# One core, one layer: the forgetting gate moved into the second score product, and four smaller edits

## The chip, the core and the metric

The kernel runs on one core of one Trainium2 chip. The metric is device time in microseconds, from the program's start to its end. Three runs of the kernel before took 779.17, 785.84 and 786.11 us, so the median is 785.84 us. A core has a matmul engine (PE, whose weight loads are listed apart as PEld), a vector engine (DVE), a scalar engine (ACT), GpSimd (POOL) and a queue engine (SP), and each works through its own list of instructions in order.

## The reference

One layer of a streaming encoder on 512 positions of width 1024, in float32. Three sub-layers, each with an RMS norm before and after it: a token mixer, cross-attention into 256 memory rows, and a SwiGLU block of width 2816. The mixer has 8 heads of forgetting attention (fox) and 8 heads of chunked attention with a learned relative bias. The change touches the fox heads and the SwiGLU block.

```python
# fox head: q, k, v are 512 x 64; log_f is the logarithm of a sigmoid gate, one per head and position
c = cumsum(log_f)
s = q @ k.T / 8 + c[:, None] - c[None, :]          # and -1e30 where the key is later than the query
p = softmax(s); out = p @ v
# SwiGLU
g, u = split(h @ w_gate_up)                          # 1024 -> 2 x 2816
y = (silu(g) * u) @ w_down
```

## The kernel before

**Two-part numbers.** Every large product is made of float32 values held as a high part (rounded to the PE's fast format) and a low part (the rest). `mm3` (lines 139 to 142) issues three matmuls for one product: high by high (L140), high by low (L141) and low by high (L142). ACT makes the high parts and DVE the low parts, also of all weights that arrive by DMA.

**Order.** The Python code is written in the order of the algorithm, and a scheduler puts the instructions of each engine in order, by a priority that runs on with the code. `later(n)` shifts the priority of what stands in it, so that one stage's work is drawn between another's. The built program has one fixed list per engine; a wait holds up all that stands behind it on that engine.

**Stages.** The first stage (0 to 35 us) computes V of the fox heads while x and its weights arrive: `x_block`, `v_weights` and `squares` prepare 128 rows of features at a time, `v_products` uses them. The loop at L237 gives PE six small matmuls on a zeroed tile before any data is there. Sums of squares run over POOL (L289) and DVE (L321, L322). `vhi` and `vlo` hold the weights, in a part of 264 columns and one of 256 columns.

**Heads.** Four groups of four heads follow (35 to 245 us). `group_proj` computes Q and K of a group; its matmuls are PE's filler between the steps of the heads. `fin_q` writes Q with the high part of a head in one half of the 128 rows (`own`) and the low part in the other (`other`). `fin_k` writes T with the high part of K in both halves, and L with the low part of K in `own` and zeros in `other` (the zeros come from POOL, L383 and L384, once for each of three tiles in `klz`). So a head's score is two matmuls: Q by T (L515) gives high by high and low by high, and Q by L (L516) gives high by low. `forget_gate` computes c for all eight heads, as high and low rows in `c40`, and its columns in `ct`. `fox_bias` then makes, for each fox head, one matmul that spreads the row -c over 128 partitions (L480), four ACT steps that add the column c (L485) and four POOL steps that write the causal mask (L486). `head` adds that bias to the score while it looks for the row's maximum (DVE, L519), exponentiates (ACT, L529), divides (L530, L531), transposes (PE, L534), splits into two parts again (L536, L537) and multiplies by V (L543).

**SwiGLU.** Blocks of 256 columns of gate and up, u = 0 to 10. Block 0 is `first_ffn`. Of the others, three halves run as `eight` (eight plain products of 128x512x256) and seventeen as `seven` (seven products of sums, Strassen's way). `product` is the common piece: four times `mm3` with 256 columns. Weights pass through a ring (`ring_hi`, `ring_lo`, lines 902 and 903) that `take` fills as far ahead as its slots are free. The down projection follows (663 to 775 us). There, `mm` can cut the third matmul of one `mm3` in two (`cuts`, L1226 to L1229), which happens once in each half:

```python
            for part in (slice(0, cut), slice(cut, to.stop - to.start)):
                pe.matmul(dst[:, part], lhs[1], rhs[0][:, part], start=False, stop=end)
```

## Time and profile before

| | |
|---|---|
| runs shown | 779.17, 785.84, 786.11 us |
| profiled execution | 786.02 us, span 784.1 us from the first to the last instruction |
| PE busy | 763.6 us (97%), 4996 matmuls |
| DVE, ACT, POOL busy | 597.9, 429.7, 70.9 us |
| chain that ended last | PE 81%, ACT 6%, DVE 5% |

A matmul's record is longer than the time it takes from its neighbours, because matmuls overlap: 256 columns show as 0.28 us, but the next one starts after 0.11 or 0.12 us. So PE's speed is read from the starts, or from the number of matmuls in a stretch. The profiled execution is close to the median of the runs.

### The profile page before, as it was taken

The page shows a single profiled execution, that of the slowest core. Times are in us where ns is not written, and L with a number is a line of the kernel's source. Part 1 is how long each engine was busy: PE and PEld are TensorE (multiplying, and loading weights), DVE is VectorE, ACT ScalarE, POOL GpSimd, SP SyncE. Part 2 cuts the span into 40 slices and gives each one's busy share as a digit, 9 for nine tenths or more (in the row PEclk, how much of TensorE's full clock was granted, in tenths as well). Part 3 has the DMA queues.
Part 4 walks back from the last instruction along what each step waited for, and adds up shares of the span by engine and source line. Part 5 has one row for each costly group of instructions (what it writes and reads, how often), then busy time and mean ns, then how long its engine had stood idle before and what let it go on. Part 6 is the DMA issues. An engine that isn't in the chain of part 4 may idle for free.

```text
span 784.1 us, 12865 instructions
## 1 busy us (share of the span) xinstructions
PE 763.6 (97%) x4996; PEld 683.5 (87%) x4996; DVE 597.9 (76%) x1089; ACT 429.7 (55%) x781; POOL 70.9 (9%) x110
## 2 busy tenths in 40 slices
PE   8899999999999999999999999999999999999996
PEld 8887788888778988877778899999999999898985
DVE  5567889879887588645563778998899998987736
ACT  7358888757886348444553635554344446454421
POOL 6001231110321101000001100000000000000001
PEclk9999999999999999999999999999999999999999
DMA  6241212412312734421350202332433332323222
GB/s 245 79 137 54 55 55 67 130 67 82 114 60 96 276 107 163 131 72 64 107 171 18 81 28 81 108 109 81 135 109 108 108 109 77 111 92 124 89 74 107
DMA packets 60748, 80.05 MB, mean 102 GB/s; under 512 B 2704, under 2 KB 43664, under 8 KB 60688
## 3 DMA queue, kind: packets, MB, share of 16 engines
q1 hardware_dynamic: 59264, 74.49, 29.5%
q0 software_dynamic: 1280, 4.72, 1.6%
q8 instruction: 39, 0.64, 0.3%
q14 instruction: 21, 0.17, 0.1%
q10 hardware_dynamic: 144, 0.02, 0.0%
HBM read 77.13 MB, written 2.10 MB: 101 GB/s over the span
## 4 chain that ended last, share of the span: by engine, by line
PE 81%; ACT 6%; DVE 5%; issue 3%; DMA 2%; POOL 2%; SPq 0%; DVEq 0%; POOLq 0%; ACTq 0%
PE ps_a L141 15%; PE ps_a L142 15%; PE ps_a L140 15%; PE ps_s L140 5%; PE ps_s L141 5%; PE ps_s L142 5%; PE ps_t L141 2%; PE ps_t L140 2%; PE ps_t L142 2%; PE ps_o L140 2%; PE ps_o L141 2%; PE ps_o L142 2%; PE ps_t L534 2%; DMA raw<-in_dram 2%; PE ps_o L543 2%
## 5 line engine op out<-in xcount | busy, mean ns | idle before, releaser
L902 ACT CAST ring_hi<-fraw 128x1024 fp32r<-128x1024 f32 (+1 forms) x62 | 57.5, 931 | 65.1 <-DVE fraw L981 16.2
L126 DVE TENSOR_TENSOR lo<-raw,hi 128x1024 fp32r<-128x1024 f32 x56 | 68.2, 1223 | 22.2 <-ACT hi L125 21.8
L903 DVE TENSOR_TENSOR ring_lo<-fraw,ring_hi 128x1024 fp32r<-128x1024 f32 (+1 forms) x62 | 66.4, 1074 | 18.4 <-ACT ring_hi L902 17.9
L142 PE MATMUL ps_a<-hTh,lo 128*128 128x512 f32 x192 | 76.8, 400 | 0.6 <-DVE lo L126 0.6
L140 PE MATMUL ps_a<-hTh,hi 128*128 128x512 f32 x192 | 75.8, 395 | 0.2 <-ACT hi L125 0.2
L141 PE MATMUL ps_a<-hTl,hi 128*128 128x512 f32 x192 | 75.9, 395 | 0.0
L125 ACT CAST hi<-raw 128x1024 fp32r<-128x1024 f32 x56 | 57.8, 1048 | 23.8 <-PE ps_a L141 15.0
L902 ACT CAST ring_hi<-sums 128x1024 fp32r<-128x1024 f32 x34 | 35.7, 1049 | 52.5 <-PE ps_t L141 17.0
L903 DVE TENSOR_TENSOR ring_lo<-sums,ring_hi 128x1024 fp32r<-128x1024 f32 x34 | 41.4, 1218 | 4.0 <-ACT ring_hi L902 4.0
L142 PEld LDWEIGHTS ps_a<-hTh,lo 128*128 128x128 f32 x192 | 36.1, 188 | 7.3 <-DVE lo L126 1.0
L141 PEld LDWEIGHTS ps_a<-hTl,hi 128*128 128x128 f32 x192 | 36.1, 188 | 6.4
L140 PEld LDWEIGHTS ps_a<-hTh,hi 128*128 128x128 f32 x192 | 36.2, 188 | 6.0 <-ACT hi L125 0.4
L529 ACT ACTIVATE p<-p,nm 128x128 f32<-128x128 f32 (+1 forms) x64 | 36.1, 565 | 8.4 <-DVE nm L519 7.6
L140 PE MATMUL ps_a<-b,ring_hi 128*128 128x256 f32 x140 | 39.4, 281 | 0.0
L141 PE MATMUL ps_a<-b,ring_hi 128*128 128x256 f32 x140 | 39.3, 281 | 0.0
L142 PE MATMUL ps_a<-b,ring_lo 128*128 128x256 f32 x140 | 39.3, 281 | 0.0
L140 PE MATMUL ps_s<-b,ring_hi 128*128 128x256 f32 x128 | 36.0, 281 | 0.0
L141 PE MATMUL ps_s<-b,ring_hi 128*128 128x256 f32 x128 | 36.0, 281 | 0.0
L142 PE MATMUL ps_s<-b,ring_lo 128*128 128x256 f32 x128 | 36.0, 281 | 0.0
L536 ACT CAST pth<-ps_t 128x128 fp32r<-128x128 f32 (+1 forms) x64 | 27.1, 425 | 14.5 <-PE ps_t L534 13.7
L537 DVE TENSOR_TENSOR ptl<-ps_t,pth 128x128 fp32r<-128x128 f32 (+1 forms) x64 | 30.7, 486 | 5.1 <-ACT pth L536 3.8
L534 PE MATMUL ps_t<-ident,p 128*128 128x128 f32 x160 | 28.1, 275 | 1.1 <-DVE p L531 0.8
(541 smaller groups left out, 2642.5 us busy)
## 6 DMA issues: line engine op xcount, KB each, us to landing
raw<-in_dram SPq DMA_DIRECT2D x64, 512.0 KB, 3.7
fraw<-in_dram SPq DMA_DIRECT2D x62, 512.0 KB, 3.5
cb<-in_dram SPq DMA_DIRECT2D x8, 256.0 KB, 2.7
xo<-in_dram POOLq DMA_DIRECT2D x4, 512.0 KB, 5.4
out_dram<-yd SPq DMA_DIRECT2D x8, 256.0 KB, 2.0
rawv<-in_dram SPq DMA_DIRECT2D x3, 520.0 KB, 6.9
xt<-in_dram SPq DMA_DIRECT2D x3, 512.0 KB, 7.7
gb<-in_dram POOLq DMA_DIRECT2D x3, 512.0 KB, 4.4
```

Of the source, the lines that this page charges most:

```text
L125: act.copy(hi[:, j : j + n, :], raw)
L126: dve.tensor_tensor(out=lo[:, j : j + n, :], in0=raw, in1=f32(hi[:, j : j + n, :]), op=ALU.subtract)
L140: pe.matmul(dst, sh, mh, start=first, stop=False)
L141: pe.matmul(dst, sh, ml, start=False, stop=False)
L142: pe.matmul(dst, sl, mh, start=False, stop=last)
L529: act.activation(p[:, :n], p[:, :n], AF.Exp, bias=nm, scale=-1.0, accum_out=sm)
L534: pe.transpose(tp[:, k * P : (k + 1) * P], p[:, k * P : (k + 1) * P], ident)
L536: act.copy(span(ph, i), t3)
L537: dve.tensor_tensor(out=span(pl, i), in0=t3, in1=f32(span(ph, i)), op=ALU.subtract)
L543: pe.matmul(acc[:, a:], v[:, k, vh, :], m[:, k * PTS + a : k * PTS + SEQ], start=k == 0 and m is ph, stop=k == NT - 1 and m is pl,)
L902: act.copy(h2, v)
L903: dve.tensor_tensor(out=l2, in0=v, in1=f32(h2), op=ALU.subtract)
```

## The change

The diff makes five edits.

1. The gate goes into the second score product. The zero half of L takes the rows of `c40` (`gate_rows`, ACT), and the left operand of that product becomes a new tile `ql` (`fox_left`): the high part of Q in `own`, and in `other` a column of -1 in the rows that hold this head's c (two ACT steps of 64x512 for each head). The column c is left out, since the softmax of a row doesn't depend on it. One causal mask serves all heads. `fox_bias`, `ct` and its transposes are gone. The zeros of L are written when the chunked heads need them.
2. The loop before the data arrives has ten matmuls in place of six.
3. The 256-column part of `vhi` and `vlo` starts 48 elements into its tile.
4. ACT uses Exp once right after the gate's Ln, and Silu once at the end of cross-attention.
5. In gate blocks u = 1, 2, 4 and 7, the third matmul of the first `product` is cut into two of 128 columns.

```diff
-        for j in range(6):
+        for j in range(10):
...
-        vhi = [wp.tile([P, KB, n], F32R, tag="hi", name=f"vhi{n}", bufs=2) for n in (264, 256)]
-        vlo = [wp.tile([P, KB, n], F32R, tag="lo", name=f"vlo{n}", bufs=2) for n in (264, 256)]
+        def v_part(tag, n, skip):
+            t = wp.tile([P, skip + KB * n], F32R, tag=tag, name=f"v{tag}{n}", bufs=2)
+            return t[:, skip:].rearrange("p (k n) -> p k n", k=KB)
+
+        vhi, vlo = ([v_part(tag, n, skip) for n, skip in ((264, 0), (256, AS_MOVING))] for tag in ("hi", "lo"))
...
-            pool.memset(f32(l[H1, 0, :]), 0.0)
-            pool.memset(f32(l[H0, 1, :]), 0.0)
...
+                if 4 < nkl[0] <= 4 + len(klz):
+                    pool.memset(f32(l[H1, 0, :]), 0.0)
+                    pool.memset(f32(l[H0, 1, :]), 0.0)
...
+            act.activation(warm, u[:, :1], AF.Exp)
...
-            sel = cst.tile([P, 8], F32R, tag="sel", name="sel")
-            pool.memset(f32(sel), 0.0)
-            for r in (0, 32):
-                dve.tensor_scalar(
...
-            ct = cst.tile([P, NT, 8], F32, tag="ct", name="ct")
...
-                pe.transpose(tp[:, t * 8 : (t + 1) * 8], c[:, t * P : (t + 1) * P], ident[0:8, 0:8])
-            dve.tensor_copy(ct, tp[:, : NT * 8].rearrange("p (t h) -> p t h", t=NT))
-            return c40, sel, ct
 
-        def fox_bias(h, c40, sel, ct):
-            acc = bank("s")
-            pe.matmul(acc, sel[:, h : h + 1].to_broadcast([P, P]), c40, start=True, stop=True)
...
-                t = bp.tile([P, SEQ], F32, tag="bi", name=f"fb{h}_{i}", bufs=4)
-                act.activation(t[:, :n], acc[:, :n], AF.Identity, bias=ct[:, i, h : h + 1])
-                pool.affine_select(
...
-                tiles.append(t[:, :n])
-            return tiles
+            return c40
...
+        sel = cst.tile([P, 8], F32, tag="sel", name="sel")
+        dve.memset(sel, 0.0)
+        for r in (0, 32, 64, 96):
+            dve.tensor_scalar(
+                out=sel[r : r + 8, :], in0=ident[r : r + 8, r : r + 8], scalar1=-1.0, scalar2=None, op0=ALU.mult
+            )
+        causal = bp.tile([P, SEQ], F32, tag="causal", name="causal")
+        pool.memset(causal, 0.0)
+        pool.affine_select(
...
+        masks = [causal[:, SEQ - (i + 1) * P :] for i in range(NT)]
+
+        def gate_rows(l, c40, h):
+            act.copy(l[(H1, H0)[h], h, :], c40[H0, :])
+
+        def fox_left(q, h, hh):
+            own, other = ((H0, H1), (H1, H0))[h]
+            t = bp.tile([P, SEQ], F32R, tag="bi", name=f"ql{hh}", bufs=4)
+            act.copy(t[own, :], f32(q[own, h, :]))
+            act.activation(t[other, :], ones[other, :].to_broadcast([64, SEQ]), AF.Copy, scale=sel[other, hh : hh + 1])
+            return t
...
-        def head(q, kt, kl, v, vh, h, bias, o):
+        def head(q, ql, kt, kl, v, vh, h, bias, o):
...
                 pe.matmul(s[:, :w], q[:, h, ts], kt[:, h, :w], start=True, stop=False)
-                pe.matmul(s[:, :w], q[:, h, ts], kl[:, h, :w], start=False, stop=True)
+                pe.matmul(s[:, :w], ql[:, ts], kl[:, h, :w], start=False, stop=True)
...
-                        bias = fox_bias(hh, *gate) if side == 0 else chunk_bias(hh)
+                        if n == 0 and b == 0:
+                            gate_rows(klz[0], gate, h)
+                        if side == 0:
+                            bias, ql = masks, fox_left(q[b], h, hh)
+                        else:
+                            bias, ql = chunk_bias(hh), q[b][:, h, :]
+                    if n == 0 and h == 1:
+                        with later(urge[n]):
+                            for other in range(2):
+                                gate_rows(klz[b + 1], gate, other)
                     with later(urge[n]):
-                        head(q[b], kt[b], kl[b], v, 2 * b + h, h, bias, o)
+                        head(q[b], ql, kt[b], kl[b], v, 2 * b + h, h, bias, o)
...
+        act.activation(mix_ms[:, 0, 0:1], sm[:, :1], AF.Silu)
...
-        def product(dst, w, b, first=True, last=True):
+        def product(dst, w, b, first=True, last=True, parts=(slice(0, 256),)):
             for k in range(4):
-                mm3(dst, w[0][:, k, :], w[1][:, k, :], b[:, 0, k, :], b[:, 1, k, :], first and k == 0, last and k == 3)
+                if k:
+                    parts = (slice(0, 256),)
+                pe.matmul(dst, w[0][:, k, :], b[:, 0, k, :], start=first and k == 0, stop=False)
+                pe.matmul(dst, w[0][:, k, :], b[:, 1, k, :], start=False, stop=False)
+                for to in parts:
+                    pe.matmul(dst[:, to], w[1][:, k, :], b[:, 0, k, to], start=False, stop=last and k == 3)
+        IN_STEP = (slice(0, P), slice(P, 256))
...
-                        product(accs[m][:, ns], w, bs[n], half == 0 and n == 0, half == 1 and n == 1)
+                        begin = half == 0 and n == 0
+                        product(accs[m][:, ns], w, bs[n], begin, half == 1 and n == 1, *([parts] if begin and m == 0 else []))
...
-            product(p17[:, left], a11, b11)
+            product(p17[:, left], a11, b11, parts=parts)
...
+            whole, parts = (slice(0, 256),), IN_STEP if u in (1, 2, 4, 7) else (slice(0, 256),)
             if 2 * u in EIGHT:
-                eight(("a", "a"), gate_eight)
+                eight(("a", "a"), gate_eight, parts)
             else:
-                seven(G, ("a", "a", "a", "o"), gate_seven)
+                seven(G, ("a", "a", "a", "o"), gate_seven, parts)
...
             else:
-                seven(U, ("s", "s", "t", "t"), up_seven(dst))
+                seven(U, ("s", "s", "t", "t"), up_seven(dst), whole)
```

The built lists show the change at three places. The first is POOL in the first stage, from the zeroing of L to the last sum of squares (`xs`). Before:

```order
L383 MEMSET L_412 64x512
L384 MEMSET L_412 64x512
L289 TENSOR_TENSOR xs<-xs 128x512
L383 MEMSET L_415 64x512
L289 TENSOR_TENSOR xs<-xs 128x512
L384 MEMSET L_415 64x512
L383 MEMSET L_418 64x512
L289 TENSOR_TENSOR xs<-xs 128x512
L384 MEMSET L_418 64x512
L289 TENSOR_TENSOR xs<-xs 128x512
L454 MEMSET fzero 8x512
```

Now:

```order
L478 MEMSET causal 128x512
L459 MEMSET fzero 8x512
L292 TENSOR_TENSOR xs<-xs 128x512
L479 AFFINE_SELECT causal<-causal 128x128
L292 TENSOR_TENSOR xs<-xs 128x512
L463 MEMSET c_615 128x512
L292 TENSOR_TENSOR xs<-xs 128x512 x2
```

Between the second and the last of the sums, four zeroing steps of L have gone, and one mask step (`causal`) and the zeroing of `c40` stand there.

The second place is PE and ACT at the first fox head. `ps_s` are scores, `ps_a` the projection that fills in. PE before:

```order
L480 MATMUL ps_s_624<-c_605,sel 128x512
L515 MATMUL ps_s_646<-T_542,Q_468 128x256
L516 MATMUL ps_s_646<-L_412,Q_468 128x256
L142 MATMUL ps_a_1042<-hTh,lo_506 128x512
L140 MATMUL ps_a_1074<-hTh,hi_505 128x512
L141 MATMUL ps_a_1074<-hTl,hi_505 128x512
L142 MATMUL ps_a_1074<-hTh,lo_506 128x512
L140 MATMUL ps_a_1074<-hTh,hi_505 128x512
L141 MATMUL ps_a_1074<-hTl,hi_505 128x512
L515 MATMUL ps_s_661<-T_542,Q_468 128x256
L516 MATMUL ps_s_661<-L_412,Q_468 128x256
L142 MATMUL ps_a_1074<-hTh,lo_506 128x512
```

and now:

```order
L140 MATMUL ps_a_1003<-hTh,hi_514 128x512
L141 MATMUL ps_a_1003<-hTl,hi_514 128x512
L518 MATMUL ps_s_627<-L_416,ql_624 128x256
L518 MATMUL ps_s_642<-L_416,ql_624 128x256
L142 MATMUL ps_a_1003<-hTh,lo_515 128x512
L140 MATMUL ps_a_1003<-hTh,hi_514 128x512
L517 MATMUL ps_s_658<-T_551,Q_477 128x384
L518 MATMUL ps_s_658<-L_416,ql_624 128x384
L141 MATMUL ps_a_1003<-hTl,hi_514 128x512
L142 MATMUL ps_a_1003<-hTh,lo_515 128x512
L140 MATMUL ps_a_1003<-hTh,hi_514 128x512
```

The matmul L480 is gone, Q by T of the first two tiles has moved ahead (it isn't shown), and L by `ql` waits for ACT's rows. ACT before:

```order
L459 CAST c_605<-fc 8x512
L485 ACTIVATE fb_0_626<-ps_s_624,ct 128x128
L485 ACTIVATE fb_1_631<-ps_s_624,ct 128x256
L485 ACTIVATE fb_2_636<-ps_s_624,ct 128x384
L485 ACTIVATE fb_3_641<-ps_s_624,ct 128x512
L529 ACT_TABLE_LOAD
L529 ACTIVATE p_0_649,sm_651<-p_0_649,nm_650 128x128
L406 ACTIVATE Q_1069<-qk 64x512 x2
L529 ACTIVATE p_1_664,sm_666<-p_1_664,nm_665 128x256
```

and now:

```order
L464 CAST c_615<-fc 8x512
L491 COPY L_416<-c_615 64x512 x2
L491 COPY L_417<-c_615 64x512
L531 ACTIVATE p_0_630,sm_632<-p_0_630,nm_631 128x128
L491 COPY L_417<-c_615 64x512
L491 COPY L_418<-c_615 64x512
L531 ACTIVATE p_1_645,sm_647<-p_1_645,nm_646 128x256
L538 CAST pth_408<-ps_t_638 128x128
L491 COPY L_418<-c_615 64x512
L497 ACTIVATE ql_1114<-ones,sel 64x512
```

In place of four bias steps and a table load stand six copies of the gate's rows, three of them ahead of the first exponential.

The third place is PE at the start of gate block u = 2 (`b` is the activation, `ring` the weights). Before:

```order
L142 MATMUL ps_s_4961<-b_4272,ring_lo 128x256
L140 MATMUL ps_a_5072<-b_4271,ring_hi 128x256
L141 MATMUL ps_a_5072<-b_4271,ring_hi 128x256
L142 MATMUL ps_a_5072<-b_4271,ring_lo 128x256
L140 MATMUL ps_a_5072<-b_4271,ring_hi 128x256
L141 MATMUL ps_a_5072<-b_4271,ring_hi 128x256
L142 MATMUL ps_a_5072<-b_4271,ring_lo 128x256
```

and now:

```order
L1086 MATMUL ps_s_4822<-b_4132,ring_lo 128x256
L1083 MATMUL ps_a_4933<-b_4131,ring_hi 128x256
L1084 MATMUL ps_a_4933<-b_4131,ring_hi 128x256
L1086 MATMUL ps_a_4933<-b_4131,ring_lo 128x128 x2
L1083 MATMUL ps_a_4933<-b_4131,ring_hi 128x256
L1084 MATMUL ps_a_4933<-b_4131,ring_hi 128x256
L1086 MATMUL ps_a_4933<-b_4131,ring_lo 128x256
```

The third matmul has become two of 128 columns; nothing else moved there. At u = 4 and 7 it is the same. At u = 1 four transposes stand between the halves, and the rest of block 0's matmuls come after them.

## Rows read from the trace of the kernel before

**Rows 1.** The page: busy time of each engine, and the chain that ended last

```profile
PE 763.6 (97%) x4996; PEld 683.5 (87%) x4996; DVE 597.9 (76%) x1089; ACT 429.7 (55%) x781; POOL 70.9 (9%) x110
...
PE 81%; ACT 6%; DVE 5%; issue 3%; DMA 2%; POOL 2%; SPq 0%; DVEq 0%; POOLq 0%; ACTq 0%
```

**Rows 2.** Windows: stretch, its length, busy time and count by engine, granted clock, DMA

```profile
60.00:150.00 90.00, 87.28 (x491) 72.61 (x490) 76.69 (x209) 75.91 (x176) 18.51 (x41) 1.00 0.25 71
483.85:663.34 179.49, 179.49 (x1526) 179.49 (x1525) 164.43 (x238) 87.84 (x132) 0.00 (x0) 1.00 0.32 103
564.41:643.43 79.02, 79.02 (x673) 79.02 (x672) 74.77 (x108) 37.40 (x56) 0.00 (x0) 1.00 0.33 105
686.20:708.90 22.70, 22.70 (x203) 22.70 (x202) 18.58 (x30) 12.37 (x18) 0.00 (x0) 1.00 0.34 116
```

**Rows 3.** Timeline of PE, first stage: start, length, what, idle before and its end

```profile
1.05 2.93 PE L237 MATMUL ps_t<-rrow 128*128 128x128 f32 x12 [1.05 <-DVE mhalf L82]
...
5.67 0.78 PE L140 MATMUL ps_s<-vhi,hTh 128*128 128x264 f32 x2 [1.70 <-DVE vhi L271]
...
20.27 0.39 PE L141 MATMUL ps_s<-vlo,hTh 128*128 128x264 f32 x1 [1.06 <-DVE vlo L275]
```

**Rows 4.** Timeline of POOL and of DVE, first stage

```profile
17.11 0.52 POOL L384 MEMSET L<- 64x512 f32 x1
17.59 1.28 POOL L289 TENSOR_TENSOR xs<-xs 128x512 f32<-128x512 f32 x1
...
15.27 0.73 DVE L281 SCALAR_TENSOR_TENSOR hTl<-xt,gn,hTh 128x512 fp32r<-128x512 f32 x1
18.91 0.69 DVE L322 TENSOR_TENSOR xs<-xs 128x512 f32<-128x512 f32 x1 [2.90 <-POOL xs L289]
```

**Rows 5.** Timeline of PE at the first fox head

```profile
59.79 0.41 PE L474 MATMUL ps_t<-ident,fc 8*128 8x8 f32 x4 [0.30 <-DVE fc L456]
60.13 0.50 PE L142 MATMUL ps_a<-hTh,lo 128*128 128x512 f32 x1
...
64.34 0.40 PE L480 MATMUL ps_s<-c,sel 128*128 128x512 f32 x1
64.58 0.28 PE L515 MATMUL ps_s<-T,Q 128*128 128x256 f32 x1
...
69.01 0.50 PE L515 MATMUL ps_s<-T,Q 128*128 128x512 f32 x1 [1.22 <-DVE nm L519]
```

**Rows 6.** Timeline of ACT at the first fox head

```profile
64.78 1.78 ACT L485 ACTIVATE fb<-ps_s,ct 128x128 f32<-128x128 f32 x4 [1.96 <-PE ps_s L480]
66.58 1.28 ACT L529 ACT_TABLE_LOAD   x1
67.88 0.40 ACT L529 ACTIVATE p<-p,nm 128x128 f32<-128x128 f32 x1
```

**Rows 7.** Lines L485 and L422 on ACT: count, ns least, median and most

```profile
L485 ACT ACTIVATE fb<-ps_s,ct x32: 346/524/717, 64.8 to 133.0; 128x128 f32<-128x128 f32 x8, 128x256 f32<-128x256 f32 x8, 128x384 f32<-128x384 f32 x8, 128x512 f32<-128x512 f32 x8
...
L422 ACT CAST T<-qk x16: 607/618/622, 53.2 to 209.4; 64x512 fp32r<-64x512 f32 x16
```

**Rows 8.** Waits of PE for the bias: us in total, times, longest

```profile
PE ps_s L515 <- ACT fb L485: 1.0, 2, 0.7
```

**Rows 9.** Timeline of PE in block 0 of SwiGLU

```profile
455.45 0.41 PE L141 MATMUL ps_a<-b,gate_w 128*128 128x256 f32 x2
455.70 0.28 PE L142 MATMUL ps_a<-b,gate_w 128*128 128x256 f32 x1
```

**Rows 10.** Timeline of PE at the cut in the down projection

```profile
685.25 0.28 PE L1227 MATMUL ps_s<-ring_lo,latex 128*128 128x256 f32 x1
685.36 0.33 PE L1229 MATMUL ps_s<-ring_hi,latex 128*128 128x128 f32 x2
...
685.82 0.28 PE L142 MATMUL ps_s<-ring_hi,latex 128*128 128x256 f32 x1
685.94 0.28 PE L140 MATMUL ps_a<-ring_hi,latex 128*128 128x256 f32 x1
```

More of the change, by code (lines that the diff above doesn't have):

```diff
@@ L472, in forget_gate @@
-            tp = bank("t")
-            for t in range(NT):
-                pe.transpose(tp[:, t * 8 : (t + 1) * 8], c[:, t * P : (t + 1) * P], ident[0:8, 0:8])
-            dve.tensor_copy(ct, tp[:, : NT * 8].rearrange("p (t h) -> p t h", t=NT))
-            return c40, sel, ct
-        def fox_bias(h, c40, sel, ct):
-            acc = bank("s")
-            pe.matmul(acc, sel[:, h : h + 1].to_broadcast([P, P]), c40, start=True, stop=True)
-            tiles = []
-            for i in range(NT):
-                n = (i + 1) * P
-                t = bp.tile([P, SEQ], F32, tag="bi", name=f"fb{h}_{i}", bufs=4)
-                act.activation(t[:, :n], acc[:, :n], AF.Identity, bias=ct[:, i, h : h + 1])
-                pool.affine_select(
-                    out=t[:, i * P : n],
-                    in_=t[:, i * P : n],
-                    pattern=[[-1, P]],
-                    compare_op=ALU.is_ge,
-                    fill=NEG,
-                    base=0,
-                    channel_multiplier=1,
-                )
-                tiles.append(t[:, :n])
-            return tiles
+            return c40
@@ new lines, in hybrid_block_kernel @@
+        sel = cst.tile([P, 8], F32, tag="sel", name="sel")
[7 more added lines that the diff above has]
+        pool.affine_select(
+            out=causal[:, SEQ - P :],
+            in_=causal[:, SEQ - P :],
+            pattern=[[-1, P]],
+            compare_op=ALU.is_ge,
+            fill=NEG,
+            base=0,
+            channel_multiplier=1,
+        )
@@ L1081, in up_eight, with eight @@
             return done
-        def eight(tags, done):
+        def eight(tags, done, parts):
             accs = [bank(tag) for tag in tags]
@@ L1118, in twice, with seven @@
             return bass.AP(a.tensor, a.offset, [list(a.ap[0]), [0, 2], list(a.ap[-1])])
-        def seven(O, tags, done):
+        def seven(O, tags, done, parts):
             p17, p26, p35, p4 = (bank(tag) for tag in tags)
```

8 lines of the change are left out of this document (1 added, 7 removed).

## The prediction

> **What bounds the kernel now.** I read the page first: PE is busy for 97% of the span and holds 81% of the chain that ended last [rows 1]. So a microsecond off another engine is worth something only where PE waits for it, and what counts is how fast PE goes through its own list. The waits come next: those of PE for the bias, which the change removes, are 1.0 us in all [rows 8]. Then the windows, where the speed of PE shows. In SwiGLU blocks 2 to 10 the stretch of 179.49 us holds 1526 matmuls of 256 columns; two of these were still running at its start, so 1524 started, one every 117.8 ns. In the down projection, 22.70 us hold 203 of the same size, so 200 or 201 started: 112.9 to 113.5 ns, I use 113.3. The granted clock is 1.00 in both [rows 2]. **The same matmul has two speeds**, and neither stretch has a wait in it. The timeline shows where they change. In block 0, one matmul starts late (two records from 455.45, then 455.70, 0.25 us for two) and the slow stretch begins [rows 9]. In the down projection the first 256-column matmuls stand ahead of the cut, at 685.25 and 685.36 the first half of the third; from 685.82 on a matmul starts every 0.11 to 0.12 us, and the 113.3 ns are those of the 200 behind it [rows 2, 10]. So the trace of before already contains the cut that the change puts into SwiGLU, with the same two halves, and the fast pace behind it. The three runs differ by 6.9 us, which is about what the slow pace costs in blocks 1 to 10; I take that as a hint that an execution can fall on either pace, no more.
>
> **Edit 5, the cuts.** Up to u = 2 nothing changes: the cut at u = 1 stands ahead of the rest of block 0, where the pace was lost. From the start of u = 2 (483.85) to the end of gate and up, 1524 matmuls at 113.3 in place of 117.8 give -6.9 us. A cut itself costs: from 685.25 to 685.94 there are 0.69 us for what five matmuls do in 0.57 [rows 10], so 0.12 us, three times: +0.4. Net **-6.5 us**. Bounds: +0.5 (the pace doesn't change, four cuts paid) and -7.6: block 1 fast too, from 455.70 [rows 9] to 483.85 some 28.15 / 0.1178 = 239 matmuls at 4.5 ns less, -1.1. The cover is DVE, which makes the weights' low parts. In its densest four blocks it is busy 74.77 of 79.02 us [rows 2]; at the fast pace these last 79.02 x 113.3 / 117.8 = 76.0 us. It still fits, with 1.2 us to spare, so I put no new wait here. If the cover goes, DVE's 74.8 us is the floor, and the loss is small.
>
> A rule speaks against this edit. The Trainium skill, page "TensorE: Matmul & The Clock Gate", section "Back-to-back issue gap", gives the warm distance of isolated matmuls as columns / 2.4 + 2.5 ns; nothing but the columns stands in it. By it, as an estimate, 256 columns take 109.2 ns wherever they stand, two halves 55.8 each, and four cuts would cost 10 ns and bring nothing. The trace differs: 117.8 and 113.3 ns at one clock [rows 2].
>
> **Edit 1, the gate, on PE.** Eight matmuls L480 go. The first takes from 64.34 to the next start at 64.58, 0.24 us, so 8 x 0.24 = -1.9 us. The transposes of c go: from the first, at 59.79, to the projection's next matmul at 60.13 are 0.34 us, and PE was idle for 0.30 ahead of them, so -0.6 [rows 5]. The waits for the bias go: -1.0 [rows 8]. At the first head, ACT needs 1.78 us for four bias steps and 1.28 us for a table, and the first exponential starts at 67.88 [rows 6]. Now three copies of 64x512 stand ahead of it, 0.62 us each by the row of a step of that shape [rows 7], 1.9 us from c's arrival (no later than 64.34, where L480 starts without a wait). It can start at about 66.2, 1.7 us earlier; 0.24 + 0.64 of that is already counted in PE's own list, so -0.8. PE's wait of 1.22 us at 69.01 [rows 5] I leave where it is: the new order has the same work ahead of it. Sum -4.3.
>
> **Edit 1, what it adds.** ACT gets 16 steps for ql and 6 for the rows, 22 x 0.62 = 13.6 us, and loses 32 bias steps at a median of 0.524, 16.8 us [rows 7]. It is lighter by 3 us, and it has 14 us idle in the 90 us of this stretch [rows 2]: no cost. The steps for ql wait until PE has read the tile's former content. In the built list they stand right behind a step that waits for PE's row next to it, so I give that nothing, and keep it as a rival. POOL loses its 32 mask steps and is idle anyway. DVE loses one copy. The zeros of L, now for the chunked heads, are six POOL steps of 0.52 us [rows 4] on an engine that is busy for 18.5 of the 90 us [rows 2]. DVE is busy for 76.7 of the 90 us and the heads' chains run through it, so I expect some of PE's gain to come back as waits for DVE: **-4.0 us**, bounds 0 and -5.5 (the whole 1.22 at 69.01 as well).
>
> **Edits 2 to 4.** Ten loop matmuls: twelve records take from 1.05 to 3.98 [rows 3] and six matmuls make twelve, so twenty take 4.9 and end at 5.9 at the latest, against 5.67 for PE's first real matmul. If PE then starts at full clock, it runs the first 128 features faster, but it meets the wait at 20.27 [rows 3] all the same. That wait hangs on DVE, which sits 2.90 us until POOL's last sum ends at 18.87 [rows 4]. Four zeroings of L (0.52 each, 2.1 in all) are gone between the sums; a mask step and a zeroing come in. At the 0.52 of a zeroing they take 1.0 and the sum ends 1.0 us earlier; at the 1.28 of a sum they take 2.6 and it ends 0.5 later. They are nearer to the first. One hTl step (0.73) moves from before the sum to behind it [rows 4], and ACT has one ql step (0.62) among its casts. I take half of the wait of 1.06, -0.5. The 256-column part of V is at most 96 matmuls, and what its place in the tile can do is bounded by the two paces, 4.5 ns for each: 0 to -0.4, I take -0.2. Together **-0.7 us**, bounds +0.6 (the hTl or the ql step on the path) and -1.5. Exp's table load moves off the first head (counted above) to a place where ACT is ahead of need. Silu's moves to where ACT has nothing due: 0, covered by the whole of block 0.
>
> **Sum.** 786.02 - 6.5 - 4.0 - 0.7 = **774.8 us**, against the profiled execution, which stands 0.18 us above the median shown. That is 1.4% less.
>
> **Rivals.**
> A. *The cuts don't set the pace*, or it is lost again soon after: the longest fast stretch in the rows is the 200 matmuls of the down projection. For it: nothing shows a cut in a stretch that has been slow for long. Against: the stretch behind the one cut shown kept the fast pace to its end. Time: 786.0 + 0.5 - 4.0 - 0.7 = 781.8. The page of the Trainium skill named above would have it so.
> B. *DVE takes the heads' gain.* DVE at 85% there [rows 2]; the chain of a head is DVE, ACT, DVE, PE, so PE waits where it used to multiply. Against: PE is busy 87.3 of 90 us, filler is there. Time: 786.0 - 6.5 - 0.5 - 0.7 = 778.3.
> C. *ACT's list is held by ql, and it is slower than before.* There are four tiles for ql, so the steps for heads 5 to 8 wait until PE has finished the scores of the head four before; the exponentials stand behind them. If the list is such that each costs a whole head's scores (from the first, at 64.58, to the end of the one at 69.01 after 0.50: 4.9 us [rows 5]), that is +19.7: 774.8 + 19.7 = 794.5. It turns the result from 2.8 us per head on. Against: the waits in the built list are for rows that PE reaches just before.
>
> **Chances.** Forecast 0.68 (own range 771 to 778), A 0.16, B 0.10, C 0.06. Downwards the range goes to the bounds of all terms, 786.0 - 7.6 - 5.5 - 1.5 = 771.4, upwards it takes in B and A: **771.0 to 782.0**. About 1%, 7.9 us, is what a measurement of this kernel can tell from no change. Faster by more, below 778.1: nearly all of the forecast and some of B, 0.69. Within: the rest of these and A, 0.26. Slower: C, 0.05.
>
> **What would show it.** In the changed profile, gate and up from u = 2 must hold a matmul every 113 ns; if it is 118 from there on, A. If it is 113 at first and 118 later, the place of the change names what undoes it, and u = 4 and 7 are tries to mend it. L480 and L474 must be gone, the first exponential must follow the first score by less than 2 us, and PE's waits for DVE between 60 and 150 us must not have grown by more than 1 us (else B). A wait of ACT for PE ahead of a ql step, longer than 1 us and in four heads, would be C. DVE's wait for POOL at 18.9 must be shorter. I am wrong altogether if PE waits inside gate and up: then the fast pace has outrun DVE, and a wait may cost the pace as well.

## The result and the profile after

Twenty runs of the changed kernel took 780.08 to 784.01 us, median 782.33; twenty of the kernel before 779.17 to 789.06, median 786.2. The ratio is **0.9949, interval 0.9938 to 0.9960**: 0.5% faster, where 1.4% was forecast, and 0.3 us above the range. The profiled execution took 782.23 us, with a span of 780.5. Beside the kernel before on another chip (after_again, below) the same kernel came to 0.9987 [0.9959, 1.0016]. Why the two measurements differ is half of the answer.

The times of the kernel before fall into two groups. Of its 161 runs on all chips together 77 lie at 785.38 us or above, 84 at 784.05 or below, and none between; by chip 19 of 20 (the first measurement), 17 of 35, 13 of 35, 13 of 29, 6 of 19, 9 of 23 lie above. The changed kernel has none of its 30 runs there. Below, the upper group means the runs from 785 us on.

The page of the changed kernel: busy time, and the chain that ended last [rows 1].

```profile
PE 757.2 (97%) x4996; PEld 675.7 (87%) x4996; DVE 599.0 (77%) x1091; ACT 429.4 (55%) x773; POOL 60.9 (8%) x79
PE 69%; DVE 13%; ACT 10%; issue 4%; DMA 3%; POOL 1%; SPq 0%; DVEq 0%; POOLq 0%; ACTq 0%
```

PE is still busy for 97%, but DVE and ACT now hold 23% of the chain, against 11%: more of the chain runs through them. The windows of the changed kernel (stretch, length, busy time and count of PE, PEld, DVE, ACT, POOL, granted clock, DMA) [rows 2]:

```profile
60.00:150.00 90.00, 86.58 (x484) 71.29 (x483) 78.99 (x210) 71.34 (x159) 10.70 (x15) 1.00 0.25 71
455.70:483.80 28.10, 28.10 (x241) 28.10 (x240) 22.06 (x24) 10.90 (x13) 0.00 (x0) 1.00 0.21 64
485.30:616.20 130.90, 130.90 (x1157) 130.90 (x1156) 121.37 (x174) 62.25 (x93) 0.00 (x0) 1.00 0.34 105
641.10:658.80 17.70, 17.70 (x152) 17.70 (x152) 16.39 (x27) 9.68 (x18) 0.00 (x0) 1.00 0.30 102
```

Two matmuls run at the start of each stretch, so the pace is 28.10 / 239 = 117.6 ns ahead of the cut at u = 2, 130.90 / 1155 = 113.3 ns behind it, as forecast, and 17.70 / 150 = 118 in the last 18 us. (In a short window this division is off by a few tenths of a ns.) The granted clock is 1.00 in all of them. In the heads PE is idle for 3.4 of the 90 us, before for 2.7, and DVE is busier. PE's waits (us in total, times, longest):

```profile
PE ps_t L536 <- DVE p L533: 2.4, 3, 1.4
PE ps_s L141 <- DVE vlo L278: 1.7, 2, 1.0
PE ps_s L517 <- ACT T L430: 1.5, 2, 1.1
...
PE ps_a L142 <- DVE lo L126: 1.3, 1, 1.3
...
PE ps_s L1083 <- ACT v L1147: 0.7, 1, 0.7
...
PE ps_s L141 <- DVE ring_lo L915: 0.4, 1, 0.4
```

The waits for the bias [rows 8] are gone; those for p, T and lo are new or longer, and two stand in SwiGLU and the down projection, where PE did not wait before. Where they are on PE's timeline:

```profile
36.29 0.50 PE L142 MATMUL ps_a<-hTh,lo 128*128 128x512 f32 x1 [1.29 <-DVE lo L126]
...
55.61 0.51 PE L517 MATMUL ps_s<-T,Q 128*128 128x256 f32 x2 [1.08 <-ACT T L430]
...
138.87 0.52 PE L536 MATMUL ps_t<-ident,p 128*128 128x128 f32 x3 [1.41 <-DVE p L533]
...
617.12 0.39 PE L1083 MATMUL ps_s<-tlo,ring_hi 128*128 128x256 f32 x1 [0.69 <-ACT v L1147]
...
697.86 0.38 PE L141 MATMUL ps_s<-ring_lo,latelo 128*128 128x256 f32 x1 [0.41 <-DVE ring_lo L915]
```

The next table shows where time went. It compares the starts of the same matmul (the same occurrence of its operands) in two traces: negative is earlier than in the profiled execution of the kernel before, in us. The columns are the matmuls that start there at about 36.6 (the first heads' projection), 150, 430, 664 (the start of the down projection) and 750 us. The kernels of the experiments are explained below.

| kernel | 36.6 | 150 | 430 | 664 | 750 |
|---|---|---|---|---|---|
| the change | 0.0 | -0.4 | -0.3 | -4.4 | -3.7 |
| after_again | +2.1 | +1.8 | +2.1 | -4.8 | -3.5 |
| e5_only | -0.5 | -0.5 | -0.7 | -6.2 | -4.6 |
| no_e5 | +0.1 | -0.1 | -0.2 | -8.0 | -8.0 |
| e1_again | +1.8 | +1.9 | +2.0 | -4.6 | -3.9 |
| e234_only | +0.8 | -0.7 | +0.1 | -7.0 | -4.2 |
| cut_u1 | -0.4 | -0.4 | -0.1 | +0.4 | +0.4 |
| cut_quarter | -0.2 | -0.2 | +0.5 | +0.6 | +0.6 |
| cut_u2 | -0.2 | -0.2 | +0.7 | -6.9 | -6.0 |
| cut_late1 | -0.3 | -0.2 | +0.3 | -5.7 | -4.5 |
| pool_s3 | +0.6 | +0.5 | +0.7 | -1.3 | +0.4 |
| no_s3 | +1.8 | +1.7 | +2.7 | -4.4 | -4.4 |
| ql_first | +1.7 | -1.9 | -1.3 | -8.4 | -7.0 |
| best | +1.7 | -1.9 | -2.2 | -9.0 | -7.7 |
| best_again | +2.2 | -1.3 | -0.8 | -8.5 | -8.1 |
| sel_late | -1.7 | -3.4 | -3.1 | -8.8 | -7.4 |

### The profile page after: what moved, and what is told of

It is laid out like the page before. It is cut to its first block, busy times and chain, and to the rows that moved or that the text cites. A ratio compares the mean times of both kernels' runs of the same rounds, so it can differ in the third digit from the quotient of the medians.

```text
span 780.5 us, 12777 instructions
## 1 busy us (share of the span) xinstructions
PE 757.2 (97%) x4996; PEld 675.7 (87%) x4996; DVE 599.0 (77%) x1091; ACT 429.4 (55%) x773; POOL 60.9 (8%) x79
## 4 chain that ended last, share of the span: by engine, by line
PE 69%; DVE 13%; ACT 10%; issue 4%; DMA 3%; POOL 1%; SPq 0%; DVEq 0%; POOLq 0%; ACTq 0%
PE ps_a L141 10%; PE ps_a L140 9%; PE ps_a L142 9%; PE ps_a L1086 3%; PE ps_a L1083 3%; PE ps_a L1084 3%; PE ps_s L1083 3%; PE ps_s L1086 3%; PE ps_s L1084 3%; DMA raw<-in_dram 2%; PE ps_s L141 2%; PE ps_s L142 2%; PE ps_s L140 2%; DVE lo L126 2%; PE ps_t L536 2%
## 5 line engine op out<-in xcount | busy, mean ns | idle before, releaser
L1086 PE MATMUL ps_a<-b,ring_lo 128*128 128x256 f32 (+1 forms) x144 | 39.3, 276 | 0.0
L1168 ACT ACTIVATE G<-G 128x256 f32<-128x256 f32 x36 | 14.0, 414 | 33.0 <-DVE G L1153 15.6
```

Of the source, the lines that this page charges most:

```text
L1086: pe.matmul(dst[:, to], w[1][:, k, :], b[:, 0, k, to], start=False, stop=last and k == 3)
```

## The experiments

Each is compared with runs of the kernel before on the same chip. Times scatter by 3 us and more within a group, so the counts, the profiles and the table often say more than a median.

**The edits apart.** e5_only has the kernel before with `IN_STEP` and the cuts alone, no_e5 the change with

```diff
-            whole, parts = (slice(0, 256),), IN_STEP if u in (1, 2, 4, 7) else (slice(0, 256),)
```

and all that hangs on it undone; e1_only has the gate's edit alone, e234_only the other three.

e5_only: 

> The kernel before with edit 5 alone (the third matmul of the first product cut in two at u = 1, 2, 4, 7). Theory: nearly all that the change gained is the pace of PE in gate and up, less what the fast pace pays back behind it: a wait of 0.7 us for ACT's copy v near the end, the pace lost again for the last block, a wait of 0.4 for a weight's low part in the down projection. Then this kernel gains what the whole change gains, 3.5 to 4.5 us, 782 us against 786.2. Rival: the gate's edit and edits 2 to 4 carry half of it. Then 784 or more. If the pace pays nothing back without the other edits, 6.5 us, 779.7.

Measured: 780.53 us (778.80 to 781.87, 12 runs), 0.9964 [0.9930, 0.9997]; none of 12 in the upper group. Its windows ahead of and behind the cut at u = 2 give 28.00 / 238 = 117.6 and 130.50 / 1151 = 113.4 ns:

```profile
456.00:484.00 28.00, 28.00 (x240) 28.00 (x240) 21.61 (x24) 12.52 (x15) 0.00 (x0) 1.00 0.23 70
485.30:615.80 130.50, 130.50 (x1153) 130.49 (x1152) 121.46 (x175) 62.34 (x95) 0.00 (x0) 1.00 0.35 106
```

no_e5: 

> The change without edit 5. Theory: what edits 1 to 4 take off PE's list it waits for a little later, so 785.5 to 786.2, a ratio of 0.999 to 1.000, and all of gate and up from 455 us on at one matmul in 117.8 ns. Rival: the gate's edit is worth its 4 us, and it was the cuts that brought little: 782.

Measured: 780.20 us (777.87 to 788.10), 0.9963 [0.9926, 0.9999], 1 of 12 in the upper group. The expectation fell, and in an unforeseen way: with no cut at all, the profiled execution (778.02 us) is at the fast pace from block 0 to the end. A window of it:

```profile
456.00:655.00 199.00, 199.00 (x1759) 199.00 (x1757) 185.00 (x260) 98.98 (x145) 0.00 (x0) 1.00 0.33 102
```

199.00 / 1757 = 113.3 ns. So the pace is not a property of the kernel; an execution takes one or the other. The change itself shows both ahead of its cut at u = 2: 117.6 ns in its first profile, and 113 in after_again (25.00 us hold 223 matmuls from 459 on). The two groups of times fit that: the profiled execution of the kernel before, 786.02 us, was slow throughout [rows 2], and no fast one of it was profiled.

e1_only: 

> The kernel before with edit 1 alone (the gate in the second score product). Theory: eight matmuls, four transposes and the waits for the bias go (3.4 us of PE), and waits for T, for p and for L at the same places take most of it back: at the end of the heads (the first V product of the cross-attention or the last of the 512-column projections near 150 us) PE is 0 to 1 us ahead of the kernel before, and the time is 785.3 to 786.3. Prediction's value: 782.2.

Measured: 780.9 us, 0.9970 [0.9928, 1.0013], 4 of 11 runs in the upper group. A twelfth execution, the profiled one, took 1934 us, and its 128x512 matmuls show as 0.84 us, against 0.39 to 0.50. The cause is not known and nothing is read from it; e1_again is the same kernel once more, for a profile.

e234_only: 

> The kernel before with edits 2, 3 and 4 alone (ten still matmuls, the 256-column part of V at offset 48, Exp and Silu used early). Theory: V ends some 0.7 us earlier, but the wait at 36.3 us for the low part of the first projection weights grows by as much, so nothing is left: 786.0 to 786.4, and that wait is 1.2 us or more in place of 0.6. Rival: that wait grew for another reason (edit 1's steps on DVE or ACT), and here the 0.7 stay: 785.4.

Measured: 780.91 us, 0.9986 [0.9946, 1.0026], 2 of 12 in the upper group. In the table it enters the projection 0.8 us late and gains 1.5 us in the heads, with Exp's table loaded early and the old bias; and PE's wait of 1.22 us at 69.01 [rows 5] is gone. Edit 4 is the only one of the three that acts in the heads, so the gain is likely its own.

e1_again: 

> The kernel before with edit 1 alone once more, for the profile alone. Theory: from 36 to 150 us PE gains under 1 us on the kernel before; with the table load of Exp still at the first exponential, the wait for T at 55 us, a wait of the first head for its exponentials and the one for p near 139 are there. Prediction's value: 4 us gained.

Measured: 782.06 us, one run. In the heads it gains nothing (+1.8 to +1.9). Two of PE's waits:

```profile
PE ps_t L532 <- DVE p L529: 2.4, 3, 1.4
PE ps_s L513 <- DVE nm L517: 1.9, 4, 1.3
```

**The pace.** cut_u2 and cut_u1 are e5_only with one cut each:

```diff
-IN_STEP if u in (1, 2, 4, 7) else
+IN_STEP if u == 2 else
```

(`u == 1` in cut_u1); cut_quarter is cut_u2 with

```diff
-        IN_STEP = (slice(0, P), slice(P, 256))
+        IN_STEP = (slice(0, 64), slice(64, 256))
```

and cut_late1 cuts the first product of the second column block in u = 1 (`begin and m == 1`), which stands behind the rest of block 0.

cut_u2: 

> The kernel before with one cut, in the first product of u = 2, and nothing else of the change. Theory (the kernel before runs at one of two paces from block 0 on, by chance, and a cut puts PE back on the fast one): from the cut at 484 us on a matmul starts every 113.3 ns whatever the pace was ahead of it, no run lies at 785 us or above, and with only one cut's cost the median is 778.5 to 780.5. Rival 1 (it takes all four cuts): some runs at 785 or above. Rival 2 (the waits of the cut kernels near 617 and 698 us come from the other cuts or from the fast pace itself): with them here too, 780.5 to 782.

cut_late1: 

> The kernel before with one cut, in u = 1, in the first product of its second column block, which stands behind the rest of block 0, some 28 matmuls before the end of that product's turn (near 461 us). Theory: the fast pace starts there, 23 us earlier than behind a cut at u = 2, which is worth 1.0 us in those executions in which the pace was lost in block 0; no run at 785 us or above, median 777.7 to 779.7. Rival (a cut undoes a slow pace only by chance of its place): runs at 785 or above, as before.

cut_u1: 

> The kernel before with the cut at u = 1 alone, where the change has it: that product is pulled ahead of the rest of block 0, so the cut stands at 450 us, ahead of the place at 455 us where the profiled executions lost the pace. Theory: it protects nothing, and of 12 runs 3 to 9 lie at 785 us or above, as in the kernel before. Rival (any cut, or any change of the list, ends the slow executions): none at 785 or above.

cut_quarter: 

> The kernel before with one cut at u = 2, into 64 and 192 columns in place of 128 and 128. Theory (a short matmul shifts the loads against the matmuls, and PE settles on the fast pace): no run at 785 us or above, median 779 to 781, as with 128 and 128. Rival (the halves have to be equal): 3 to 9 of 12 runs at 785 or above.

| kernel | median, range (12 runs) | ratio | upper group |
|---|---|---|---|
| cut_u2 | 780.17, 779.06 to 783.71 | 0.9973 [0.9943, 1.0004] | 0 of 12 |
| cut_late1 | 780.76, 778.65 to 781.99 | 0.9973 [0.9941, 1.0005] | 0 of 12 |
| cut_u1 | 782.31, 779.17 to 787.01 | 0.9992 [0.9956, 1.0027] | 5 of 12 |
| cut_quarter | 780.48, 779.15 to 786.62 | 0.9978 [0.9944, 1.0012] | 2 of 12 |

cut_u1 protects nothing, as expected: its profiled execution is slow from 456 us to the end. A window of it, and two of cut_quarter's profiled execution (786.62 us), ahead of and behind its cut:

```profile
456.00:663.00 207.00, 207.00 (x1760) 207.00 (x1760) 185.80 (x260) 99.84 (x146) 0.00 (x0) 1.00 0.31 98
```

```profile
456.00:484.00 28.00, 28.00 (x240) 28.00 (x240) 22.40 (x24) 12.18 (x14) 0.00 (x0) 1.00 0.21 63
486.00:663.00 177.00, 177.00 (x1506) 177.00 (x1505) 162.34 (x236) 85.98 (x131) 0.00 (x0) 1.00 0.33 102
```

207.00 / 1758 is 117.7 ns; cut_quarter has 117.6 ahead of the cut and 177.00 / 1504 = 117.7 behind it: **the cut into 64 and 192 columns left the slow pace as it was**, against the theory. That is one execution; by the counts alone, 2 of 12 are not told apart from 0 of 12. A cut into two equal halves was seen to end it three times: in the change, in e5_only, and in sel_late (below), whose windows are

```profile
453.00:481.00 28.00, 28.00 (x240) 28.00 (x239) 21.88 (x23) 10.97 (x14) 0.00 (x0) 1.00 0.21 64
482.50:630.00 147.50, 147.50 (x1304) 147.50 (x1303) 138.51 (x201) 70.52 (x105) 0.00 (x0) 1.00 0.34 104
```

117.6 ahead of its one cut and 113.3 behind it. In cut_u2 and cut_late1 the profiled executions came to the cut at the fast pace already, so for them only the counts speak. Over all kernels that have an equal cut behind 455 us (without pool_s3, which waits), none of 112 runs lies in the upper group. Kernels without one have between 1 of 12 (no_e5) and 5 of 12 runs there (cut_u1).

The cut is not the only thing that changes the pace. e1_again, which has no cut, was fast from 458 us and became slow near 641, about where the change did. Its windows give 113.3 and 117.5 ns:

```profile
486.00:635.00 149.00, 149.00 (x1317) 149.00 (x1317) 140.09 (x202) 72.38 (x107) 0.00 (x0) 1.00 0.34 106
641.20:656.00 14.80, 14.80 (x128) 14.80 (x127) 13.53 (x20) 8.40 (x15) 0.00 (x0) 1.00 0.24 81
```

And in pool_s3 (below) a slow stretch of 6 us ended at a wait of 0.37 us at 644.5, with no cut there. So a delay can do either, and the runs do not say which.

**What the fast pace costs.** pool_s3 and no_s3 take one sum of the weights off DVE:

```diff
-                dve.tensor_tensor(out=s3, in0=lower[:, :, :P], in1=lower[:, :, P:], op=ALU.add)
+                pool.tensor_tensor(out=s3, in0=lower[:, :, :P], in1=lower[:, :, P:], op=ALU.add)
```

in pool_s3. In no_s3 an `if n < 8:` ahead of the DVE line leaves the sum out in thirteen of its seventeen places.

pool_s3: 

> The whole change, with one of the four sums of weights in each seven-product half (s3, 128x512, 0.68 us on DVE, 17 times) on POOL in place of DVE. Theory: at the fast pace DVE has no time left, so that one late load stays a deficit to the end, and PE meets it as waits near 617 and 698 us and a lost pace at 641. With some 11 us less on DVE the low parts stand 6 us or more ahead of use, the three places are gone, and this gains 1.5 to 2.2 us on the whole change: the profiled span is 778.5 or less in place of 780.5. Rival (those waits are ACT's, which gets its weights late from the DMAs): the wait near 617 stays, gain under 0.7. Against both: POOL takes longer for a sum and the loads wait for it: slower.

Measured: 786.74 us (785.60 to 788.37), 1.0047 [1.0014, 1.0079]: slower, as the last of the three cases. Not from the slow pace, but from waits; two rows of PE's waits and two of POOL's timeline:

```profile
PE ps_a L1086 <- DVE ring_lo L915: 1.5, 3, 0.6
PE ps_s L1086 <- DVE ring_lo L915: 1.4, 2, 0.9
```

```profile
518.80 1.30 POOL L944 TENSOR_TENSOR sums<-fraw 128x512 f32<-128x512 f32 x1 [9.17 <-DVE ring_lo L915]
529.73 1.68 POOL L944 TENSOR_TENSOR sums<-fraw 128x512 f32<-128x512 f32 x1 [9.63 <-DVE ring_lo L915]
```

In these rows a sum takes POOL 1.3 and 1.7 us for DVE's 0.68, and the low parts come later, not earlier. So it did not test the theory.

no_s3: 

> The whole change; from the ninth block half of gate and up on (n = 8), the sum s3 of weights is left out (0.68 us of DVE each, about 9 us in all), so the weights of two products are old ones there. Theory (at the fast pace DVE sets when the low parts are there, and ACT's list stands behind DVE's): with the 9 us off DVE the low parts stand 5 us or more ahead of their use to the end of gate and up, PE waits neither near 617 nor near 698 us, and the pace is not lost: the profiled span is 778.0 to 779.0, the median 2 us below the change's 782.3 or at 778 to 780. Rival (the waits hang on loads and on ACT's copy v, not on DVE): the waits near 617 and 698 us stay at 0.4 us or more each, and the span is 780 or more.

after_again: 

> The change itself once more, for a second profile and times beside the kernel without s3. Theory: behind the cut at 484 us the pace is 113.3 ns again; near 616 and 697 us PE waits again, 0.3 to 1 us each, since DVE is as full as in the first profile. Median 779 to 782.5, no run at 785 or above. Rival (the waits came from one late load in that one execution): no wait in gate and up, and under 0.3 us near 697.

Measured, on one chip: no_s3 780.75 us (779.04 to 782.96, 10 runs), 0.9983 [0.9950, 1.0017]; after_again 781.72 (778.98 to 783.40, 10 runs), 0.9987 [0.9959, 1.0016]. In no_s3 PE waits for no weight in SwiGLU or the down projection: its starts are -4.4 us at 664 and -4.4 at 750, and the low parts stand 3.4 us or more ahead of their use all through gate and up, against 1.7 us at the least in after_again (and about 4.6 in the slow profile of the kernel before). after_again has no wait in gate and up, and this one of 0.64 us in the down projection:

```profile
698.10 0.38 PE L141 MATMUL ps_s<-ring_lo,latelo 128*128 128x256 f32 x1 [0.64 <-DVE ring_lo L915]
```

So the wait near 698 is for DVE's low parts, and it comes back. It is a price of the fast pace and not of the cuts: between 664 and 750 the table shows a loss of 0.7 to 2.8 us in most fast profiles, also in e1_again and e234_only, which have no cut. But no_e5 and best_again, which make the sum, lose nothing and 0.4 there, so one profile of no_s3 does not show that the sum is the cause. The wait at 617 is not settled either. In the change and in e5_only DVE waited for the same load at about 529, here in the change:

```profile
529.87 0.69 DVE L941 TENSOR_TENSOR sums<-fraw,fraw 128x512 f32<-128x512 f32 x1 [1.52 <-DMA fraw<-in_dram]
```

cut_late1 had that wait too (2.15 us) and waited 0.44 at the matmul of 617; but sel_late had it (2.00 us) and did not wait there, and e234_only waited 0.21 there though its DVE waited for no load near 529. That the late load is the cause is not shown.

The expected spans (778.0 to 779.0) were missed for a reason outside SwiGLU: these executions were 2 us late at 36.6, which led to the last experiment.

**The heads and the first stage.** ql_first is no_e5 with the products of the first fox head in the other order, best is the whole change with that and the cut at u = 2 alone, sel_late is best with the four steps that make `sel` behind V (a factor of -1 worked out from the gate's data holds them there).

```diff
-                pe.matmul(s[:, :w], q[:, h, ts], kt[:, h, :w], start=True, stop=False)
-                pe.matmul(s[:, :w], ql[:, ts], kl[:, h, :w], start=False, stop=True)
+                scores = [(q[:, h, ts], kt[:, h, :w]), (ql[:, ts], kl[:, h, :w])]
+                for j, (a, b) in enumerate(scores[::-1] if nhead[0] == 1 else scores):
+                    pe.matmul(s[:, :w], a, b, start=j == 0, stop=j == 1)
```

```diff
+            neg = tmp("fn")[:, :1]
+            dve.tensor_scalar(out=neg, in0=u[:, :1], scalar1=0.0, scalar2=-1.0, op0=ALU.mult, op1=ALU.add)
...
-                out=sel[r : r + 8, :], in0=ident[r : r + 8, r : r + 8], scalar1=-1.0, scalar2=None, op0=ALU.mult
+                    out=sel[r : r + 8, :], in0=ident[r : r + 8, r : r + 8],
+                    scalar1=neg[r : r + 8, :], scalar2=None, op0=ALU.mult,
```

ql_first: 

> The change without edit 5, and in the first fox head the two score products swapped: first L by ql, which needs the gate, then T by Q. Theory: what edit 1 takes off PE comes back as waits, the first of them at 55.6 us, where Q by T stands 40 matmuls ahead of L by ql and waits 1.1 us for T. With the products swapped PE does not reach T early, that wait is gone, and at 150 us PE stands 0.9 to 1.3 us earlier than in the kernel without the swap. Rival: the chain of the first head (DVE, ACT) sets the time there, and PE waits as much a few microseconds later: under 0.3 us.

Measured: 784.5 us, 0.9993 [0.9955, 1.0032], but in two groups, 776.92 to 779.15 (4 runs) and 783.47 to 784.88 (8). The medians of the two are 777.2 and 784.6; those of the kernel before on that chip are 780.1 and 786.7. At 150 us it stands 1.8 us ahead of no_e5, though it began 1.6 behind. The late start is not the reason, since after_again and e1_again began as late and gained 0.3 and nothing by 150. The waits at 55.6 and 138.9 are gone; the first head's only one is

```profile
66.45 0.39 PE L519 MATMUL ps_s<-L,ql 128*128 128x256 f32 x1 [0.48 <-ACT L L491]
```

best: 

> The whole change with two alterations: only the cut at u = 2 is kept, and in the first fox head the two score products are swapped (L by ql first). Theory: the cut keeps every execution off the slow pace, the swap takes the wait for T out of the first head. No run at 784 us or above, the fastest near 777, median 777.5 to 779.5, which is below the kernel before and below the whole change on any chip. Rival (the waits of the fast pace grow by what the heads gain): median 780 or more.

Measured: 778.37 us (774.47 to 780.16, 12 runs), **0.9924 [0.9891, 0.9958]**.

sel_late: 

> The kernel best (the change with the cut at u = 2 alone and the score products of the first head swapped), with the four steps that make sel moved behind V, by a factor -1 that is worked out from the gate's data. Theory: beside POOL's sums these steps hold DVE for 1.5 us or more at 10 to 13 us, and vlo, V and all that follow are late by it; moved, V's matmuls end 1 to 2 us earlier, PE waits for vlo under 1.5 us in all, and the median is 0.8 to 1.8 us below that of best_again, 776.5 to 777.5. Rival (the order of POOL's sums makes V late, not sel): PE's wait for vlo stays at 1.7 us or more, under 0.4 us of difference.

best_again: 

> The kernel best once more, beside sel_late: median 777.5 to 779.5, PE's wait for vlo between 1.7 and 3.7 us in all, 2.2 us or more for the steps of sel and the first vlo in DVE's list before 14 us.

Measured, on one chip: sel_late 777.48 us (776.25 to 780.02), **0.9932 [0.9903, 0.9960]**; best_again 778.60 (777.53 to 781.22), 0.9953 [0.9928, 0.9978]. DVE's timeline in best_again, POOL's there, and DVE's in sel_late:

```profile
10.02 3.81 DVE L474 TENSOR_SCALAR sel<-ident 8x8 f32<-8x8 f32 x4
13.87 0.71 DVE L278 TENSOR_TENSOR vlo<-rawv,vhi 128x528 fp32r<-128x528 f32 x1
```

```profile
10.23 1.28 POOL L292 TENSOR_TENSOR xs<-xs 128x512 f32<-128x512 f32 x1
11.47 0.28 POOL L479 TENSOR_SCALAR_AFFINE_SELECT causal<-causal 128x128 f32<-128x128 f32 x1
11.74 1.25 POOL L292 TENSOR_TENSOR xs<-xs 128x512 f32<-128x512 f32 x1
12.94 0.52 POOL L463 MEMSET c<- 128x512 f32 x1
```

```profile
10.52 2.15 DVE L278 TENSOR_TENSOR vlo<-rawv,vhi 128x528 fp32r<-128x528 f32 x2 [0.45 <-ACT vhi L276]
```

Four steps of 8x8 elements hold DVE for 3.81 us, while POOL works through its row of steps. How many of the four meet a step of POOL changes from one execution to the next. In the change three of them ran before POOL's sum, for 0.15 to 0.17 us each; the fourth began behind the sum's start and lasted nearly to its end:

```profile
10.37 1.31 POOL L292 TENSOR_TENSOR xs<-xs 128x512 f32<-128x512 f32 x1 [0.87 <-ACT xs L290]
10.54 1.17 DVE L474 TENSOR_SCALAR sel<-ident 8x8 f32<-8x8 f32 x1
```

The start of the projection follows. In three profiles (the change, no_e5, pool_s3) the four steps took 1.69 us, and it is 0.0, +0.1 and +0.6 at 36.6; in six others they took 3.3 to 3.8 us, and it is +1.7 to +2.2; with the steps moved it is -1.7. In the profile of the change they held up ACT as well, whose first `ql` step waited 1.0 us for `sel`. PE's wait for vlo is 2.9 us in best_again and 1.1 in sel_late, and the projection begins 4.0 us earlier there (+2.2 and -1.7 at 36.6). That the median falls by 1.1 only fits the table: by 430 the lead has shrunk to 2.3 and by 664 to 0.3, since this execution was slow up to its cut and best_again was not; and in the down projection sel_late loses 1.4 us at two waits for low parts.

## Why the prediction was wrong

Against the profiled execution the forecast was -11.2 us and the change gained 3.8, so 7.4 are missing. By the table, 4.4 of them are missing at 430 us (edits 1 to 4: -0.3 in place of -4.7), 2.4 in SwiGLU (-4.1 in place of -6.5), and 0.7 were lost in the down projection. The step that failed most is edit 1's -4.0.

- **The pace and the cut: right.** Two speeds at one clock, the cut at u = 2 as the switch, 113.3 ns behind it. Rival A, whose 781.8 us is nearest to the result, is refuted as a mechanism by the windows of the change, e5_only and sel_late: its number is near by luck. The Trainium skill, page "TensorE: Matmul & The Clock Gate", section "Back-to-back issue gap", gives isolated matmuls one distance for a number of columns, for 256 an estimated 109.2 ns; the windows above show two for the same matmul, 113.3 and 117.8, and the measurement decides.
- **What the cut is worth: right where the pace of 117.8 ns was taken, wrong as a gain of the kernel.** The step "1524 matmuls at 113.3 in place of 117.8 give -6.9 us" took the slow pace for the kernel's own. It is one of two that an execution falls on; the prediction had noted the hint in the three run times and drew nothing from it. Where 19 of 20 runs of the kernel before were slow, the change gained 0.5%; where 6 of 19 were, 0.1%, which is not told apart from nothing.
- **The cover by DVE: the step that failed inside edit 5.** "It still fits, with 1.2 us to spare" was made on a sum over four blocks. From 430 to 664 the change gained 4.1 of the 6.5 us. The wait of 0.69 us at 617 cost 0.9 with its restart, the pace lost again at 641 (118 ns from there) cost about as much, and some 0.4 went ahead of u = 2. And it gave 0.7 back at 698, in the down projection, where no price stood. At the fast pace the low parts of the change's two profiles stood under 2 us ahead of their use at the least, against about 4.6 in the slow profile of before; a sum of busy times over four blocks doesn't show that. Why the pace was lost at 641 stays open; e1_again lost it there too.
- **Edit 1, -4.0 us: the step that failed most, in three ways.** From 36.6 to 150 us the change gained 0.4. That is the 0.5 of rival B, but not by a full DVE: PE's waits for DVE from 60 to 150 rose from 2.0 to 2.2 us only, where B's sign was 1 us more. In all, PE's waits between 40 and 150 rose from 3.0 to 4.4 us, where the prediction took 1.0 off.

  First, "the new order has the same work ahead of it" was wrong. The wait of 1.22 us at 69.01 that it left in place is gone. But Q by T of the first two tiles had moved some forty matmuls ahead of L by `ql`, as the text on the change says, and PE now met T 1.1 us too early. With the products swapped the stretch from 36.6 to 150 gains 3.5 to 3.6 us in ql_first, best and best_again, nearly the forecast 4.0, and 1.7 in sel_late, which begins earlier and waits 2.2 us for the gate's rows at 64.7.

  Second, p at 138.9: DVE's 384-column division took 1.31 us there, beside a sum on POOL. PE's wait of 1.40 us for it stands in all six profiles with edit 1 and the old order, and in none of the four with the swap; in ql_first the sum starts 5 us behind the division. The two rows of the change, the same step in the kernel before, and in ql_first:

```profile
137.41 1.31 DVE L533 TENSOR_SCALAR p<-p,rc 128x384 f32<-128x384 f32 x1
```

```profile
136.91 1.59 POOL L565 TENSOR_TENSOR sq<-sq,o 128x512 f32<-128x512 f32 x1
```

```profile
141.58 0.42 DVE L531 TENSOR_SCALAR p<-p,rc 128x384 f32<-128x384 f32 x1
```

```profile
135.07 0.46 DVE L534 TENSOR_SCALAR p<-p,rc 128x384 f32<-128x384 f32 x1
```

  Third, "DVE loses one copy" left out that `sel`, made in two DVE steps at 23 us before, became four and a zeroing in the first stage. They are tiny, were priced at nothing, and held up vlo by up to 3 us.
- **Edits 2 to 4, -0.7 us: nothing was left of it.** V ended 0.7 us earlier in the profile of the change, and the wait for `lo` at 36.3 grew from 0.59 to 1.29; in after_again the stage came out 2.1 us later, through `sel`. The ten matmuls of edit 2 did help at first (the ten profiles with them are 0.9 to 1.8 us earlier at 12 us, of six without them one is), and then PE met vlo.
- **Rival C** did not come up: ACT waits for PE ahead of one `ql` step alone, for 0.6 us.

The Trainium skill, page "SBUF — State Buffer", section "🔬 SBUF: two separate sides", says that DVE, in some of its modes or with two inputs in SBUF, shares a pair of ports with GpSimd, that whichever starts first has it for the whole instruction, and that "the other fully blocks". The rows of `sel` and of p agree: a step of 8x8 elements took 0.15 to 0.17 us ahead of POOL's sum and 1.17 behind its start. The prediction called POOL idle and priced a DVE step by its size; by this rule and these rows neither was safe.

What stays open: why equal halves end the slow pace and 64 and 192 do not; what decides between the paces in block 0, where three profiles all have a matmul 10 to 30 ns late at the same place (two records from 455.21 to 455.45 in the change, which fell to the slow pace as the kernel before did [rows 9], and from 455.27 to 455.53 in no_e5, which did not); what the one load that DVE awaits near 529, up to 2.2 us in eight profiles, has to do with the later waits; and why the pace was lost at 641.

## What to carry to other kernels

Before a stretch's speed is put into a sum, ask whether every execution has it: times in two groups are a sign, and a profile shows one of them. A small step is not cheap by its size; look what runs beside it on the other engine (here DVE beside POOL), and who stands behind it in its list. When work leaves an engine's list, look what the scheduler draws into the gap, and whether its operands are there yet.

## What the runs showed of the hardware

- The same 256-column matmul starts every 113.3 or every 117.6 to 117.8 ns at a granted clock of 1.00, for hundreds of microseconds, and which of the two an execution takes changed between two profiles of one kernel, the change ahead of its cut.
- One cut of 128 and 128 columns ended the slow pace in all three profiles that came to it at 117.6 ns, at a cost of about 0.12 us [rows 10]; 64 and 192 left it in one of one.
- One 8x8 step on DVE took 0.15 to 0.17 us when it began ahead of POOL's sum and 1.17 when it began behind the sum's start; four took 1.69 to 3.81 us, depending on how the lists of the two engines met.
- A 128x512 sum took POOL 1.30 and 1.68 us beside a busy DVE, against 0.68 on DVE.
